# One tile per PSUM bank, and the MLP's side work dealt out over more units, in a two-layer fp32 transformer trunk

## The chip, the cores and the metric

One core of a Trainium2 chip runs the whole program once. The metric is the device time of that execution in microseconds (us), lower is better. TensorE (PE) multiplies, with its weight loads shown apart (PEld); VectorE (DVE), ScalarE (ACT) and GpSimd (POOL) do elementwise work; SyncE (SP) issues every DMA from one queue in the order written.

## The reference, cut to what matters

256 rows of width 2048 pass a forgetting attention (layer A), a squared-ReLU MLP, a shared key/value projection, a chunked attention with a relative bias (layer B) and a second MLP. All arithmetic is float32.

```python
def sq_relu_mlp(h, g, w1, w2):
    a = jax.nn.relu(rms_norm(h, g) @ w1)      # (256, 2048) @ (2048, 8192)
    return (a * a) @ w2                       # (256, 8192) @ (8192, 2048)

h = h + o.reshape(B, S, D) @ a_w_out[l]       # layer A: attention, then
h = h + sq_relu_mlp(h, mlp_norm_g[layer], mlp_w1[layer], mlp_w2[layer])
kv = rms_norm(h, kv_norm_g) @ kv_w            # shared K/V for layer B
q = (rms_norm(h, b_norm_g[l]) @ b_w_q[l])     # layer B: queries, attention, and an MLP as above
```

## The kernel before

**Units and splits.** Every weight is cut into units of 128x1024 floats: two slices of 128 input rows for 512 output columns. A unit is loaded into `raw` (four buffers), and split in `issue` into a rounded part `hi` (ACT, L183) and the rest `lo` (DVE, L184). `three` (L391 to L393) multiplies activations, split likewise, in three products: x.hi with w.hi, x.hi with w.lo, x.lo with w.hi. A unit serves 2 slices x 2 row blocks x 3 products, 12 matmuls. `hi` and `lo` have three buffers each, so when PE starts unit i, the split of unit i+2 may begin, and must be over when unit i+1 ends.

**Pairs and forms.** The MLP takes its weight columns in pairs of 1024 (halves a and b, units a0 to a7 and b0 to b7) and a chunk of 2048 hidden features at a time: chunk 0 to 3, each with two pairs of w1 and two of w2. All pairs but each MLP's first replace units 0 and 1 of both halves by seven combined units, the forms f0 to f6 (a Strassen-like product): the weights 11, T3, T2, T1, 21, T4, 22 in this order, with T1 = 12 - 11, T3 = 22 - 12, T2 = T3 + 11, T4 = 21 - T2. `bring` loads the four raw weights, `make` forms the sums on DVE (L754). A form is 6 matmuls. A pair's forms are dealt among units: f0, the last three units b5 b6 b7 of the pair before, then its own, as in f0 b5 f1 b6 f2 b7 f3 a2 f4 a3 f5 a4 f6 a5 ... b4. The form f1's product is copied to SBUF by ACT as `p` (L789), f0's to another accumulator (L786), and DVE adds `p` back twice (L767 after f2, L775 after a2). Each pair holds four PSUM banks: one pair of banks is always `acc`, the other alternately `acc` and `s`. An `acc` pair is one tile over two banks; `s` tiles have a bank each. The framework keeps order by tile: who writes a tile waits for those who still read it.

**The side work.** `fill` is a list with an entry for each unit to come (forms have none): `run_fill` runs an entry's steps after that unit's matmuls have been issued. Each 512 hidden columns, n = 0 to 3 in a chunk, go this way: after the half's last unit DVE turns the PSUM blocks into `z` (L280), SP writes `z` to DRAM (`rows`, L290) and reads it back in four parts (`columns`, L296), ACT applies ReLU (L700), squares into `hi` (L704), squares again in place (L706), DVE subtracts (L707). For n = 0, `sums` then makes the activation sums that the forms need: four DVE operations (L243 to L248), two rounded parts on ACT (L240) and two remainders on DVE (L241). Entries are counted from the unit after the one that ended the half.

**Order.** `keep_order` fixes each engine's order (DVE, ACT, PE, SP) as the code was written; nothing is reordered to fill a wait. An operation that waits holds up all behind it on its engine.

The same `sums` and `split_turned` (L257, L260, L261) split the normalised rows in `next_x` after the two output projections (stage oa and ob) and before the second layer's projections (stage qb), where `again` makes a second split for K/V.

Of the kernel before, what the change touches and what calls it, by code (L numbers as in the profile page):

```python
# [9 lines left out]
F32 = mybir.dt.float32  # L10
F32R = mybir.dt.float32r
AF = mybir.ActivationFunctionType
ALU = mybir.AluOpType
# [33 lines left out]
def trunk(ctx: ExitStack, tc: tile.TileContext, xT, xr, gs, hg, bf, wgate, w_in, w_oa, w1a, w2a,  # L47
# [159 lines left out]
    def acc_pair(which=None):  # L207
        if which is None:
            which, turns[0] = turns[0], 1 - turns[0]
        if which == 2:  # L210
            return [ps_s.tile([P, 512], F32, name="s") for _ in range(2)]
        t = ps_acc.tile([P, 2 * 512], F32, name="acc", tag=f"acc{which}", bufs=1)
        return [t[:, i * 512 : (i + 1) * 512] for i in range(2)]

    part = [None]

# [13 lines left out]
    def sums(a, fs):  # L230

        w = [wk.tile([P, 512], F32, name="sum", tag="wk") for _ in range(2)]

        def part(i):
            v = w[i // 2][:, i % 2 * 256 : i % 2 * 256 + 256].rearrange("p (g t) -> p g t", g=2)
            return v.rearrange("p g (i c) -> p g i c", i=4) if len(a[0][0].shape) == 4 else v

        def parts(i):
            hi, lo = (fs[k][:, i * 512 : (i + 1) * 512] for k in range(2))
            S.activation(hi, w[i], AF.Copy)  # L240
            V.tensor_tensor(lo, w[i], hi.bitcast(F32), op=ALU.subtract)  # L241

        V.tensor_tensor(part(0), a[1][0], a[1][1], op=ALU.add)  # L243
        V.tensor_tensor(part(1), part(0), a[0][0], op=ALU.subtract)
        parts(0)
        yield
        V.tensor_tensor(part(2), a[0][0], a[1][0], op=ALU.subtract)
        V.tensor_tensor(part(3), a[0][1], part(1), op=ALU.subtract)  # L248
        parts(1)
        yield  # L250

    def split_turned(t, n, which, into, fs=None):
# [51 lines left out]
    def next_x(n, r2, stats, which, into, kept=None, fs=None):  # L304
        add_h = residual(n, r2)
        zt = []
        fs = fs if n == 0 else None

        def use(flipped=False, which=which, into=into):
            t = zt[1].rearrange("p (i k b c) -> p k b i c", i=4, k=GH, b=NB)  # L310
            if flipped:
                t = t[:, :, :, ::-1, ::-1]
            return split_turned(t, n, which, into, fs)

        def turn():
            zt.extend(turned("s" if kept is not None and n >= 2 else "q"))
            for b in range(NB):
                blocks32(h[b][:, n * 512 : (n + 1) * 512], zt[0], b)

        def f(b, ps):  # L320
            add_h(b, ps)
            if b == NB - 1:
                step = steps(use)
                add_fill([[lambda b=b: stats.add(b, n) for b in range(NB)], [turn],
                          [lambda: add_fill(carry(*zt) + [[]] + [[step]] * (2 if fs is None else 4))]])
                if kept is not None:
                    kept.append(use)
        return f
# [101 lines left out]
        for e in evacs[2 if woven else 0 :]:  # L430
            panels(x, [e])

    def head_norm(stats, z, dst, late=0, copied=False):
        rest = []

        def f(b, ps):
            src = ps
            if copied:
                src = wk.tile([P, 512], F32, name="qc", tag="wk")
                V.tensor_copy(src, ps)  # L440
            sq = wk.tile([P, 512], F32, name="sq", tag="wk")
            S.activation(sq, src, AF.Square)
            ss = sm.tile([P, GH], F32, name="ss")
            rn = sm.tile([P, GH], F32, name="rn")

            def total():
                V.tensor_reduce(ss, sq.rearrange("p (a d) -> p a d", a=GH), axis=AX.X, op=ALU.add)

            def norm():
                vv = sm.tile([P, GH], F32, name="vv")  # L450
                V.tensor_scalar(vv, ss, 1.0 / P, stats().e[:, b : b + 1], op0=ALU.mult, op1=ALU.add)  # L451
                G.tensor_tensor(rn, vv, mhalf, op=ALU.pow)  # L452

            def turn():
                qn = wk.tile([P, 512], F32, name="qn", tag="wk")
                V.tensor_tensor(qn.rearrange("p (a d) -> p a d", a=GH), src.rearrange("p (a d) -> p a d", a=GH),
                                rn.unsqueeze(2).to_broadcast([P, GH, P]), op=ALU.mult)
                blocks32(qn, z, b)

            rest.append((total, norm, turn))  # L460
            if b == NB - 1:
                for total, norm, _ in rest:
                    total()
                    if not late:
                        norm()
                add_fill([[]] * (late - 1) + ([[n for _, n, _ in rest]] if late else []) + [[t] for _, _, t in rest] + carry(z, dst))
        return f

    def scale_q(land, layer, g):
# [93 lines left out]
    def add_fill(items):  # L563
        for i, it in enumerate(items):
            if i < len(fill):
                fill[i] = fill[i] + it
            else:
                fill.append(it)
# [126 lines left out]
    def mlp(plan, x, Sx, st, last):  # L695
# [3 lines left out]
        def take(t, c, n):  # L699
            S.activation(t, t, AF.Relu)  # L700
            y = acts.tile([P, 2, GH, T], F32R, name="act")
            hi, lo = (y[:, i].rearrange("p k (b i c) -> p (k b) i c", b=NB, i=4) for i in range(2))
            t3 = t.rearrange("p (i kb c) -> p kb i c", i=4, c=32)
            S.activation(hi, t3, AF.Square)  # L704
            yield
            S.activation(t, t, AF.Square)  # L706
            V.tensor_tensor(lo, t3, hi.bitcast(F32), op=ALU.subtract)  # L707
            hids[c].extend(y[:, :, j, :] for j in range(GH))
            yield
            if n == 0:  # L710
                room = prob.tile([P, 9 * 3 * P], F32R, name="Sh", tag="p", bufs=1)
                Sh[c].extend(room[:, i * GH * T : (i + 1) * GH * T] for i in range(2))
                yield from sums([[t3[:, 2 * j + b :: 4] for j in range(2)] for b in range(NB)], Sh[c])

        def turn_hidden(c, n):
            zt = []

            def f(b, ps):
                if b == 0:
                    zt.extend(turned())  # L720
                blocks32(ps, zt[0], b)
                if b == NB - 1:
                    step = steps(lambda: take(zt[1], c, n))
                    add_fill(carry(*zt)[:3] + [[]] + [[step]] * (4 if n == 0 else 2))
            return f

        pairs = list(dict.fromkeys(p for p, _, _ in plan))
# [1 line left out]
        def open_pair(p):  # L729
            m = pairs.index(p)  # L730
            c, second, r = m // 4, m % 4 >= 2, m % 2
            p.x, p.fs = (hids[c], Sh[c]) if second else (x, Sx)
            p.ps = [acc_pair(0), acc_pair(2 if p.third else 1)]
            if second:
                p.evac = [(last if c == NCH - 1 else residual)(2 * r + q, st.r2) for q in range(2)]
            else:
                p.evac = [turn_hidden(c, 2 * r + q) for q in range(2)]

        def bring(p, name):
            t = qkv.tile([P, UN], F32, name="w" + name, tag="kv"[name[1] == "2"], bufs=2)  # L740
# [12 lines left out]
                        "T2": ("T3", "11", ALU.add), "T4": ("21", "T2", ALU.subtract)}[name]  # L753
            V.tensor_tensor(t[name], t[a], t[b], op=op)  # L754

        ahead = {8: (bring, "12"), 7: (bring, "21"), 6: (bring, "11"), 4: (bring, "22"), 3: (make, "T1"), 2: (make, "T3")}
        starts = [i for i, it in enumerate(plan) if it[1:] == (2, 0)]
        for i, (p, q, u) in enumerate(plan):
            hi, lo = fetch()
# [8 lines left out]
            else:  # L768
# [4 lines left out]
                        p.evac[q](b, p.ps[q][b])  # L773
                if p.fast and (q, u) == (0, 2):
                    V.tensor_tensor(p.ps[1][1], p.ps[1][0], p.t["P7"], op=ALU.add)  # L775
                    make(p, "T4")
                nxt = next((j for j in starts if j > i), None)
                if nxt is not None:
                    d = sum(1 for it in plan[i:nxt] if it[1] < 2)
# [3 lines left out]
            if i and plan[i - 1][1:] in ((2, 0), (2, 1)):  # L783
                f = plan[i - 1][0]
                if plan[i - 1][2] == 0:
                    S.activation(f.ps[0][0], f.ps[1][0], AF.Copy)  # L786
                else:
                    f.t["P7"] = wk.tile([P, 512], F32, name="p7", tag="wk")
                    S.activation(f.t["P7"], f.ps[1][1], AF.Copy)  # L789

    st1, x1, S1 = RowStats("m"), [], []
    stage(o, [next_x(n, None, st1, 1, x1, fs=S1) for n in range(NG)], True)
# [2 lines left out]
    mlp(plan_a, x1, S1, st1, lambda n, r2: next_x(n, r2, st2, 3, xb, kept))  # L795
    xkv = []
    again = [steps(lambda n=n: kept[n](True, 2, xkv)) for n in range(NG)]
    add_fill([[], [], [st2.both], [], [st2.flip]] + [[]] * 13 + [[again[i // 2]] for i in range(2 * NG)])


    qs, evs = [], []
    for g in range(NG):
        box = {}

        def f(b, ps, box=box, g=g):
            if b == 0:
                z, lq = turned("z")
                box["lq"], box["f"] = lq, head_norm(lambda: st2, z, lq, copied=g == 0)
            box["f"](b, ps)
            if b == NB - 1:  # L810
                add_fill([[]] * 7 + [[lambda: qs.append(scale_q(box["lq"], 1, g))]])
        evs.append(f)
    stage(xb, evs, True)
    st2f = st2.flipped
# [90 lines left out]
```

## Time and profile before

| what | us |
|---|---|
| median of 3 runs | 2180.1 (2177.74 to 2183.59) |
| the profiled execution | 2179.85 |
| its span, first to last instruction | 2178.1 |
| PE busy (matmuls) | 2132.4 |
| weight loads busy | 1746.2 |
| DVE busy | 1571.9 |
| ACT busy | 1180.4 |

The profile's page has the busy time of each engine, the chain of waits that ended last, and groups of instructions by line. Its waits name who waited for whom; in the timeline every row has a start, a duration, the engine, the line and in brackets the idle time before it and what ended that. A matmul's row lasts 0.39 us though the next one starts 0.23 us later.

### The profile page before, as it was taken

The numbers are of one execution on the slowest core, as the hardware profiler recorded it, in microseconds if no ns is written. First come the engines' busy times: TensorE is split into PE (matmuls) and PEld (weight loads), VectorE is DVE, ScalarE is ACT, GpSimd is POOL, SyncE is SP. The second block draws the span as 40 slices with busy tenths as digits, with TensorE's granted clock in tenths as the row PEclk, the third lists the DMA queues.
The fourth block names the chain that finished last, engine by engine and source line by source line (L and its number), as shares of the span: only waits on it lengthen the run. The fifth ranks groups of instructions, "written<-read, shape, count | busy, mean of one in ns | idle before, by whom it ended". The sixth has DMA issues, their size and how long they took to land.

```text
span 2178.1 us, 25889 instructions
## 1 busy us (share of the span) xinstructions
PE 2132.4 (98%) x9338; PEld 1746.2 (80%) x9338; DVE 1571.9 (72%) x1795; ACT 1180.4 (54%) x1421; POOL 48.3 (2%) x47
## 2 busy tenths in 40 slices
PE   9999999999999999999999999999999999999999
PEld 7788887878877877878887888878788788778787
DVE  6767766677777777777766677666777777777776
ACT  6544545555465555456656444455655654565554
POOL 1100000000000000000010000000000000000000
PEclk9999999999999999999999999999999999999999
DMA  7777776766665666567668767777665666655664
GB/s 278 240 251 248 226 246 224 251 222 218 228 219 198 211 242 212 191 219 256 204 221 251 239 227 241 235 228 251 224 236 203 206 220 227 219 201 197 226 244 145
DMA packets 183889, 491.62 MB, mean 226 GB/s; under 512 B 36928, under 2 KB 73936, under 8 KB 183760
## 3 DMA queue, kind: packets, MB, share of 16 engines
q1 hardware_dynamic: 183760, 489.96, 66.7%
q8 instruction: 73, 1.20, 0.2%
q14 instruction: 56, 0.46, 0.1%
HBM read 450.01 MB, written 39.87 MB: 225 GB/s over the span
## 4 chain that ended last, share of the span: by engine, by line
PE 82%; DVE 8%; ACT 4%; issue 4%; DMA 2%; SPq 0%; ACTq 0%; DVEq 0%
PE acc L392 22%; PE acc L393 22%; PE acc L391 22%; PE s L392 5%; PE s L393 5%; PE s L391 5%; DVE lo L184 4%; ACT hi L183 2%; DVE z L280 1%; DVE w L754 1%; ACT q L700 1%; PE s L504 1%; PE po L535 1%; DMA z<-turn 1%; ACT p L789 0%
## 5 line engine op out<-in xcount | busy, mean ns | idle before, releaser
L184 DVE TENSOR_TENSOR lo<-raw,hi 128x1024 fp32r<-128x1024 f32 (+1 forms) x650 | 789.2, 1216 | 362.2 <-ACT hi L183 352.3
L183 ACT ACTIVATE hi<-raw 128x1024 fp32r<-128x1024 f32 (+1 forms) x650 | 685.6, 1056 | 523.4 <-PE acc L393 422.8
L391 PE MATMUL acc<-hi,act 128*128 128x512 f32 x2356 | 930.5, 395 | 14.1 <-ACT hi L183 14.1
L392 PE MATMUL acc<-lo,act 128*128 128x512 f32 x2356 | 924.5, 392 | 11.8 <-DVE lo L184 11.2
L393 PE MATMUL acc<-hi,act 128*128 128x512 f32 x2356 | 920.6, 391 | 0.0
L392 PEld LDWEIGHTS acc<-lo,act 128*128 128x128 f32 x2356 | 444.4, 189 | 116.5 <-DVE lo L184 26.1
L391 PEld LDWEIGHTS acc<-hi,act 128*128 128x128 f32 x2356 | 444.5, 189 | 110.6 <-ACT hi L183 18.9
L393 PEld LDWEIGHTS acc<-hi,act 128*128 128x128 f32 x2356 | 444.2, 189 | 92.2 <-DVE act L227 0.3
L183 ACT ACTIVATE hi<-w 128x1024 fp32r<-128x1024 f32 x150 | 159.1, 1061 | 223.1 <-DVE w L754 98.9
L184 DVE TENSOR_TENSOR lo<-w,hi 128x1024 fp32r<-128x1024 f32 x150 | 182.9, 1219 | 65.6 <-ACT hi L183 64.6
L392 PE MATMUL s<-lo,act 128*128 128x512 f32 x416 | 163.8, 394 | 4.3 <-DVE lo L184 4.3
L391 PE MATMUL s<-hi,act 128*128 128x512 f32 x416 | 163.3, 393 | 0.9 <-ACT hi L183 0.9
L393 PE MATMUL s<-hi,act 128*128 128x512 f32 x416 | 163.3, 392 | 0.0
L184 DVE TENSOR_TENSOR lo<-wT,hi 128x1024 fp32r<-128x1024 f32 x60 | 73.4, 1224 | 82.9 <-ACT hi L183 82.9
L183 ACT ACTIVATE hi<-wT 128x1024 fp32r<-128x1024 f32 x60 | 63.5, 1058 | 76.1 <-PE s L393 38.2
L392 PEld LDWEIGHTS s<-lo,act 128*128 128x128 f32 x416 | 79.0, 190 | 21.6 <-DVE lo L184 5.2
L391 PEld LDWEIGHTS s<-hi,act 128*128 128x128 f32 x416 | 78.8, 189 | 18.2 <-ACT hi L183 1.7
L393 PEld LDWEIGHTS s<-hi,act 128*128 128x128 f32 x416 | 79.1, 190 | 16.4
L754 DVE TENSOR_TENSOR wT<-w,w 128x1024 f32<-128x1024 f32 x60 | 73.1, 1218 | 0.0
L452 POOL TENSOR_TENSOR rn<-vv,mhalf 128x4 f32<-128x4 f32 x32 | 42.8, 1352 | 393.7 <-DVE vv L451 393.7
L538 ACT ACTIVATE act<-po 128x256 fp32r<-128x256 f32 x32 | 12.3, 385 | 67.0 <-PE po L536 67.0
L707 DVE TENSOR_TENSOR act<-q,act 128x1024 fp32r<-128x1024 f32 x32 | 39.0, 1220 | 0.5 <-ACT q L706 0.5
(161 smaller groups left out, 1337.0 us busy)
## 6 DMA issues: line engine op xcount, KB each, us to landing
raw<-in_w1a SPq DMA_DIRECT2D x100, 512.0 KB, 4.4
raw<-in_w1b SPq DMA_DIRECT2D x100, 512.0 KB, 4.2
raw<-in_w2a SPq DMA_DIRECT2D x96, 512.0 KB, 4.2
raw<-in_w2b SPq DMA_DIRECT2D x96, 512.0 KB, 4.1
raw<-in_w_in SPq DMA_DIRECT2D x94, 512.0 KB, 4.5
raw<-in_w_kv SPq DMA_DIRECT2D x64, 512.0 KB, 4.2
turn<-z SPq DMA_DIRECT2D x60, 512.0 KB, 4.2
q<-turn SPq DMA_DIRECT2D x168, 128.0 KB, 4.2
```

The costliest lines, as they stand in the source:

```text
L183: S.activation(hi[:, c], raw[:, c], AF.Copy)
L184: V.tensor_tensor(lo[:, c], raw[:, c], hi[:, c].bitcast(F32), op=ALU.subtract)
L280: V.transpose(z.rearrange("p (j n b c) -> p b n j c", j=4, n=n, b=nb)[:, b], src.rearrange("p (n j c) -> p n j c", n=n, j=4))
L391: TE.matmul(ps, xh, wh, start=first, stop=False, **kw)
L392: TE.matmul(ps, xh, wl, start=False, stop=False, **kw)
L393: TE.matmul(ps, xl, wh, start=False, stop=last, **kw)
L452: G.tensor_tensor(rn, vv, mhalf, op=ALU.pow)
L504: TE.matmul(s[:, P : 3 * P], q[:, a, P:T], k[:, a], start=True, stop=True)
L535: TE.matmul(po[:, :T], v[:, 0, a * P : (a + 1) * P], pT[:, :2], start=True, stop=False)
L700: S.activation(t, t, AF.Relu)
L707: V.tensor_tensor(lo, t3, hi.bitcast(F32), op=ALU.subtract)
L754: V.tensor_tensor(t[name], t[a], t[b], op=op)
```

## The change

The instructions are the same, and so are their numbers; only tiles, places in the fill list and the order on DVE, ACT and SP differ.

- `acc_pair` hands out two tiles of one bank where it gave one tile of two.
- `sums` issues its four additions and both ACT roundings in one step and both DVE remainders in the next.
- `take` has four steps (ReLU; square into `hi`; square in place; subtraction) where it had two; `turn_hidden` puts them at entries 3, 4, 6, 7 (n = 0, and its sums at 8, 9), 3 to 6 (n = 1), 3, 4, 6, 7 (n = 2), and 3, 4, 5, 5 (n = 3); before they stood at 4 and 5 (sums at 6, 7). `columns` follows `rows` by one entry, not two.
- `bring` and `make` come earlier, by the number of units before the next pair's f0: 12, 11, 22, 21 at 9 to 6 (were 12, 21, 11, 22 at 8, 7, 6, 4), T1 at 5 (was 3). T4 is made right after the copy of f1's product; it was made after a2 and the second addition of `p`.
- `next_x` moves the sums two entries back and n = 1's split two entries on; K/V's second splits take entries 6 to 22 in place of 18 to 25; the second layer's query group 1 turns two entries later.

```diff
-        t = ps_acc.tile([P, 2 * 512], F32, name="acc", tag=f"acc{which}", bufs=1)
-        return [t[:, i * 512 : (i + 1) * 512] for i in range(2)]
+        return [ps_acc.tile([P, 512], F32, name="acc", tag=f"acc{which}{b}", bufs=1) for b in range(NB)]
...
-        def parts(i):
-            hi, lo = (fs[k][:, i * 512 : (i + 1) * 512] for k in range(2))
-            S.activation(hi, w[i], AF.Copy)
-            V.tensor_tensor(lo, w[i], hi.bitcast(F32), op=ALU.subtract)
-
         V.tensor_tensor(part(0), a[1][0], a[1][1], op=ALU.add)
         V.tensor_tensor(part(1), part(0), a[0][0], op=ALU.subtract)
-        parts(0)
-        yield
         V.tensor_tensor(part(2), a[0][0], a[1][0], op=ALU.subtract)
         V.tensor_tensor(part(3), a[0][1], part(1), op=ALU.subtract)
-        parts(1)
+        hi, lo = ([fs[k][:, i * 512 : (i + 1) * 512] for i in range(2)] for k in range(2))
+        for i in range(2):
+            S.activation(hi[i], w[i], AF.Copy)
+        yield
+        for i in range(2):
+            V.tensor_tensor(lo[i], w[i], hi[i].bitcast(F32), op=ALU.subtract)
         yield
...
-                          [lambda: add_fill(carry(*zt) + [[]] + [[step]] * (2 if fs is None else 4))]])
+                          [lambda: add_fill(carry(*zt) + [[]] * (3 if n == 1 else 1) + [[step]] * 2 + ([] if fs is None else [[], [], [step], [step]]))]])
...
+            yield
             S.activation(hi, t3, AF.Square)
             yield
             S.activation(t, t, AF.Square)
+            yield
             V.tensor_tensor(lo, t3, hi.bitcast(F32), op=ALU.subtract)
...
-                    add_fill(carry(*zt)[:3] + [[]] + [[step]] * (4 if n == 0 else 2))
+                    uses = (4, 5, 6, 6 if late else 7) if n % 2 else (4, 5, 7, 8, 9, 10)[: 6 if n == 0 else 4]
+                    add_fill(carry(*zt, 0)[:2] + [[step] * uses.count(i) for i in range(3, uses[-1] + 1)])
...
-        ahead = {8: (bring, "12"), 7: (bring, "21"), 6: (bring, "11"), 4: (bring, "22"), 3: (make, "T1"), 2: (make, "T3")}
+        ahead = {9: (bring, "12"), 8: (bring, "11"), 7: (bring, "22"), 6: (bring, "21"), 5: (make, "T1"), 2: (make, "T3")}
...
                 if p.fast and (q, u) == (0, 2):
                     V.tensor_tensor(p.ps[1][1], p.ps[1][0], p.t["P7"], op=ALU.add)
-                    make(p, "T4")
...
                     S.activation(f.t["P7"], f.ps[1][1], AF.Copy)
+                    make(f, "T4")
...
-    add_fill([[], [], [st2.both], [], [st2.flip]] + [[]] * 13 + [[again[i // 2]] for i in range(2 * NG)])
+    add_fill([[], [], [st2.both], [], [st2.flip]])
+    slots = {6: 0, 7: 0, 8: 1, 9: 1, 13: 2, 14: 2, 21: 3, 22: 3}
+    add_fill([[again[slots[i]]] if i in slots else [] for i in range(23)])
```

Three places show what moved. The first is DVE in the second pair of w1, chunk 2 of layer A, from f3's split on (f3 splits `wT`; in the rows of before `w_6194` is weight 21 and `w_6226` becomes T4, `w_6268` is 22; a unit's split reads `raw`). Before:

```order
L184 TENSOR_TENSOR lo<-wT_6290,hi 128x1024
L767 TENSOR_TENSOR acc<-s,p_6396 128x512
L184 TENSOR_TENSOR lo<-raw,hi 128x1024
L707 TENSOR_TENSOR act<-q,act 128x1024
L280 STREAM_TRANSPOSE z<-acc 128x4x4x32 x2
L184 TENSOR_TENSOR lo<-w_6194,hi 128x1024
L184 TENSOR_TENSOR lo<-raw,hi 128x1024
L243 TENSOR_TENSOR sum<-q 128x256
L244 TENSOR_TENSOR sum<-sum,q 128x256
L241 TENSOR_TENSOR Sh<-sum,Sh 128x512
L775 TENSOR_TENSOR s<-s,p_6396 128x512
L754 TENSOR_TENSOR w_6226<-w_6194,w_6164 128x1024
```

And now, where 21 is `w_6258`, T4 `w_6196` and 22 `w_6226`, and lines past L209 stand one to four lower (L706 is the subtraction L707, L277 the turn L280):

```order
L754 TENSOR_TENSOR w_6196<-w_6258,w_6166 128x1024
L184 TENSOR_TENSOR lo<-wT_6278,hi 128x1024
L767 TENSOR_TENSOR acc<-s,p_6427 128x512
L184 TENSOR_TENSOR lo<-raw,hi 128x1024
L277 STREAM_TRANSPOSE z<-acc 128x4x4x32 x2
L184 TENSOR_TENSOR lo<-w_6258,hi 128x1024
L184 TENSOR_TENSOR lo<-raw,hi 128x1024
L775 TENSOR_TENSOR s<-s,p_6427 128x512
L184 TENSOR_TENSOR lo<-w_6196,hi 128x1024
L184 TENSOR_TENSOR lo<-raw,hi 128x1024
L706 TENSOR_TENSOR act<-q,act 128x1024
L184 TENSOR_TENSOR lo<-w_6226,hi 128x1024
```

The subtraction, the sums and T4 no longer stand between f3's split and T4's; T4 is made ahead of f3's split.

The second is ACT in the first pair of w2, chunk 2 of layer A, from f1's split (`wT`) on; f2 splits `w_6504`, and f1's product is copied to `p`. Before:

```order
L183 ACTIVATE hi<-wT_6657 128x1024
L183 ACTIVATE hi<-raw 128x1024
L786 ACTIVATE acc<-acc 128x512
L183 ACTIVATE hi<-w_6504 128x1024
L183 ACTIVATE hi<-raw 128x1024
L700 ACTIVATE q<-q 128x1024
L704 ACTIVATE act<-q 128x1024
L789 ACTIVATE p_6744<-acc 128x512
```

And now (L697 is the ReLU L700, L702 the square L704, L785 and L788 the two copies):

```order
L183 ACTIVATE hi<-wT_6692 128x1024
L183 ACTIVATE hi<-raw 128x1024
L697 ACTIVATE q<-q 128x1024
L785 ACTIVATE acc<-acc 128x512
L183 ACTIVATE hi<-w_6495 128x1024
L183 ACTIVATE hi<-raw 128x1024
L702 ACTIVATE act<-q 128x1024
L788 ACTIVATE p_6777<-acc 128x512
```

The ReLU moved ahead of f2's split, so that one pass, not two, stands ahead of the copy to `p`.

The third is DVE at the end of the second pair of w1 in chunk 0, where the sums of n = 0 have moved to (the split of `w_3897` is f0 of the first w2 pair, `wT_4062` its T3; the `raw` split ahead of the sums is b4, the one behind T3 is b5). Now:

```order
L184 TENSOR_TENSOR lo<-raw,hi 128x1024
L706 TENSOR_TENSOR act<-q,act 128x1024
L277 STREAM_TRANSPOSE z<-acc 128x4x4x32 x2
L184 TENSOR_TENSOR lo<-raw,hi 128x1024
L237 TENSOR_TENSOR sum<-q 128x256
L238 TENSOR_TENSOR sum<-sum,q 128x256
L239 TENSOR_TENSOR sum<-q 128x256
L240 TENSOR_TENSOR sum<-q,sum 128x256
L706 TENSOR_TENSOR act<-q,act 128x1024
L184 TENSOR_TENSOR lo<-w_3897,hi 128x1024
L246 TENSOR_TENSOR Sh<-sum,Sh 128x512 x2
L754 TENSOR_TENSOR wT_4062<-w_3928,w_3861 128x1024
```

Before, the sums stood two to three units earlier and one subtraction, the turn and T1 stood between b3's split and f0's; T3 followed f0's split at once. Both subtractions, the sums and their remainders now stand ahead of b5's split.

More of the change, by code (lines that the diff above doesn't have):

```diff
@@ L431, in stage, with head_norm @@
             panels(x, [e])
-    def head_norm(stats, z, dst, late=0, copied=False):
+    def head_norm(stats, z, dst, late=0, copied=False, gap=0):
         rest = []
@@ L465, in f @@
                         norm()
-                add_fill([[]] * (late - 1) + ([[n for _, n, _ in rest]] if late else []) + [[t] for _, _, t in rest] + carry(z, dst))
+                add_fill([[]] * (late - 1) + ([[n for _, n, _ in rest]] if late else []) + [[]] * gap + [[t] for _, _, t in rest] + carry(z, dst))
         return f
@@ L713, in take, with turn_hidden @@
                 yield from sums([[t3[:, 2 * j + b :: 4] for j in range(2)] for b in range(NB)], Sh[c])
-        def turn_hidden(c, n):
+        def turn_hidden(c, n, late):
             zt = []
@@ L736, in open_pair @@
             else:
-                p.evac = [turn_hidden(c, 2 * r + q) for q in range(2)]
+                p.evac = [turn_hidden(c, 2 * r + q, r == 1) for q in range(2)]
         def bring(p, name):
@@ L807, in f @@
                 z, lq = turned("z")
-                box["lq"], box["f"] = lq, head_norm(lambda: st2, z, lq, copied=g == 0)
+                box["lq"], box["f"] = lq, head_norm(lambda: st2, z, lq, copied=g == 0, gap=2 * (g == 1))
             box["f"](b, ps)
             if b == NB - 1:
-                add_fill([[]] * 7 + [[lambda: qs.append(scale_q(box["lq"], 1, g))]])
+                add_fill([[]] * (7 + 2 * (g == 1)) + [[lambda: qs.append(scale_q(box["lq"], 1, g))]])
         evs.append(f)
```

## The prediction

> **What bounds the kernel now.** First the page: the busy times, and the chain that ended last by engine.
>
> ```profile
> span 2178.1 us, 25889 instructions
> PE 2132.4 (98%) x9338; PEld 1746.2 (80%) x9338; DVE 1571.9 (72%) x1795; ACT 1180.4 (54%) x1421; POOL 48.3 (2%) x47
> PE 82%; DVE 8%; ACT 4%; issue 4%; DMA 2%; SPq 0%; ACTq 0%; DVEq 0%
> ```
>
> PE carries the chain, but 12% of it lies on DVE and ACT: at some places PE waits for a split. How much is there to win? The busy row is a poor guide, since rows overlap; the pace is a better one. In the timeline of PE in an undisturbed stretch these two rows stand nine matmuls apart:
>
> ```profile
> 769.65 0.39 PE L391 MATMUL acc<-hi,act 128*128 128x512 f32 x1
> 771.69 0.39 PE L391 MATMUL acc<-hi,act 128*128 128x512 f32 x1
> ```
>
> 2.04 / 9 = 0.227 us each, so a unit of 12 takes 2.72 and a form of 6 takes 1.36. All 9338 matmuls at that pace would be 2117; that is my estimate of the floor, 61 below the span, and a few us too high where the attention's matmuls are shorter. The Trainium skill, page "Perfetto Trace Analysis", section "Identifying the Most-Contended Engine", says likewise that matmul busy time is no good measure of the distance to roofline because matmuls are pipelined. By the busy row only 2178.1 - 2132.4 = 45.7 could be won, which would stop the gain at 2134; the trace agrees with the page, since rows of 0.39 start 0.227 apart.
>
> Next, PE's waits over the whole span (us in total, times, longest):
>
> ```profile
> PE acc L391 <- ACT hi L183: 14.1, 9, 2.1
> PE acc L392 <- DVE lo L184: 11.2, 18, 1.0
> PE acc L391 <- ACT p L789: 8.1, 8, 1.0
> ```
>
> Few and large: the timeline places nearly all of them at the same units of every chunk. A stall's price below is the distance between two starts less 0.227, which holds the restart too.
>
> **Site A, f2 of the first w2 pair, 8 times.** PE and ACT, chunk 2 of layer A:
>
> ```profile
> 828.83 0.39 PE L393 MATMUL s<-hi,act 128*128 128x512 f32 x1
> 830.23 0.50 PE L391 MATMUL acc<-hi,Sh 128*128 128x512 f32 x1 [1.01 <-ACT p L789]
> ```
> ```profile
> 825.23 1.06 ACT L183 ACTIVATE hi<-w 128x1024 fp32r<-128x1024 f32 x1 [1.17 <-PE s L393]
> ...
> 827.55 1.05 ACT L700 ACTIVATE q<-q 128x1024 f32<-128x1024 f32 x1
> ...
> 829.60 0.58 ACT L789 ACTIVATE p<-acc 128x512 f32<-128x512 f32 x1
> ```
>
> f2 writes one bank of the acc tile; f1's product sits in the other, and its copy stands behind two passes of the fill list. f2's own split (825.23 on ACT, DVE's part right behind) was over more than 2 us before. With a tile per bank f2 waits for that split alone. Its price: 1.40 - 0.227 = 1.17, and 0.1 for the restart (shown at B); the eight waits of the table above confirm the count. **8 x 1.27 = 10.2.** What hides the ReLU, now ahead of that split, is the 1.17 that ACT idles there for PE; without that cover f2's split would be 1.05 later, still ahead of its need. Next late is the first accumulator's copy, on which nothing of the next two forms hangs.
>
> **Site B, f5 of the second w1 pair, chunks 1 to 3 of both layers, 6 times.** PE, then DVE:
>
> ```profile
> 794.90 0.39 PE L393 MATMUL acc<-hi,act 128*128 128x512 f32 x1
> 797.37 0.50 PE L391 MATMUL acc<-hi,act 128*128 128x512 f32 x1 [2.09 <-ACT hi L183]
> 798.63 0.50 PE L392 MATMUL acc<-lo,act 128*128 128x512 f32 x1 [0.76 <-DVE lo L184]
> 798.97 0.40 PE L393 MATMUL acc<-hi,act 128*128 128x512 f32 x1
> ```
> ```profile
> 787.54 1.22 DVE L707 TENSOR_TENSOR act<-q,act 128x1024 fp32r<-128x1024 f32 x1
> ...
> 792.14 0.42 DVE L243 TENSOR_TENSOR sum<-q 128x256 f32<-128x256 f32 x1
> ...
> 793.72 0.69 DVE L241 TENSOR_TENSOR Sh<-sum,Sh 128x512 fp32r<-128x512 f32 x1 [0.70 <-ACT Sh L240]
> ...
> 794.93 1.22 DVE L754 TENSOR_TENSOR w<-w,w 128x1024 f32<-128x1024 f32 x1
> ```
>
> T4 is made last of all, behind the subtraction (1.22), a first addition of the sums and a second (0.42 each), a wait (0.70) and a remainder (0.69). Now T4 stands ahead of f3's split and these items, 3.45 us, come later; the stall is 2.24 + 1.03 + 0.11 = 3.38, and T4's own 1.22 leaves the place too. **6 x 3.38 = 20.3.** What DVE does later than before is late next: it has 28% of the span idle, and the sums stand at entries 8 and 9, where nothing of the same pair follows. T4 needs 21, whose load goes out one unit later (6 ahead of f0, not 7) while T4 comes some three units earlier; six units are 16 us, and the slowest landing quoted under the moved DMAs is 9.8, so I take it as landed. If DVE had no room later, the same 3.45 would stop another unit; that is the first rival.
>
> **The clock.** Behind such a stall PE can run at half pace. At two places of chunk 0 (rows under site C) and four of the six of B, rows are 0.63 long and 0.427 apart. The column behind the five engines is the granted clock:
>
> ```profile
> 462.00:473.00 11.00, 8.42 (x24) 6.12 (x23) 9.00 (x10) 4.33 (x5) 0.00 (x0) 0.69 0.62 207
> 972.00:984.00 12.00, 11.19 (x41) 8.83 (x42) 8.54 (x9) 6.39 (x8) 0.00 (x0) 0.86 0.76 246
> 1543.00:1554.00 11.00, 8.40 (x30) 6.29 (x30) 9.55 (x10) 5.64 (x7) 0.00 (x0) 0.84 0.58 201
> ```
> ```profile
> core 0: 2178.1 us, clock 0.994
> ```
>
> The mean of 0.994 gives 0.006 x 2178.1 = 13.1 us lost in all, to which chunk 0's two windows add 0.31 x 11 + 0.16 x 11 = 5.2. The other **7.9** I put to B and take as won with its stalls. It is the softest term: some of the low clock falls into the idle time itself, so it could be 5.
>
> **Site C, b4 and b5 at the end of chunk 0's second w1 pair, twice.**
>
> ```profile
> 462.61 0.39 PE L393 MATMUL s<-hi,act 128*128 128x512 f32 x1
> 463.43 0.51 PE L391 MATMUL s<-hi,act 128*128 128x512 f32 x1 [0.44 <-ACT hi L183]
> 466.08 0.79 PE L392 MATMUL s<-lo,act 128*128 128x512 f32 x1 [2.14 <-DVE lo L184]
> 466.67 0.63 PE L393 MATMUL s<-hi,act 128*128 128x512 f32 x1
> 467.09 0.63 PE L391 MATMUL s<-hi,act 128*128 128x512 f32 x1
> ```
> ```profile
> 460.06 0.42 DVE L247 TENSOR_TENSOR sum<-q 128x256 f32<-128x256 f32 x1
> ...
> 465.94 1.22 DVE L754 TENSOR_TENSOR wT<-w,w 128x1024 f32<-128x1024 f32 x1
> 467.07 1.22 DVE L184 TENSOR_TENSOR lo<-w,hi 128x1024 fp32r<-128x1024 f32 x1
> ```
>
> Before: 0.82 - 0.227 = 0.6, and 2.65 - 0.227 = 2.4, twice: 6.0, with 5.2 of clock 11.2. Here the change does not clear DVE, it regroups it. In the order now, behind b3's split, stand the subtraction, the turn, b4's split, four additions, the other subtraction, f0's split, two remainders and T3, all ahead of b5's split. Full rows of DVE start 1.13 apart (465.94 to 467.07), so: five of them (both subtractions, b4, f0, T3) 5.65, the turn about 1.2, four additions of 0.42 1.7, two remainders about 1.2, b5's split 1.2: 11.0. b3's split may begin when a7 starts, three units ahead of b4: 462.83 (462.61 + 0.227) - 3 x 2.72 = 454.7; with 1.06 on ACT, 1.23 on DVE and something queued it is over at about 457.4. Adding 11.0 and 0.5 of waiting for ACT gives 468.9; b5's remainder is needed when b4, f0 and one matmul are through: 462.83 + 2.72 + 1.36 + 0.23 = 467.1, so 1.8 late. I take 2.0 with its restart, twice 4.0, and half of the old clock loss, 2.6. Before less after: 11.2 - 6.6 = **4.6**. Both ends: no gain at all (the same backlog with another name, 0) and all of it (11.2). Page "TensorE: Matmul & The Clock Gate" of the Trainium skill, section "HAM oscillation", says that the clock is halved by idle gaps above about 3.4 us. By that rule a stall of 2 costs no clock and the sum would be 2.6 lower, 2129; the rows here show it halved behind gaps of 2.4 and 2.24, neither near 3.4, so I don't build on it.
>
> **Sites E and F, next to the attention.** PE's waits in units 5 and 6 of the last output projection (each layer), then in query group 2 and group 3 of layer B, four windows:
>
> ```profile
> PE acc L392 <- DVE lo L184: 1.5, 2, 0.9
> ```
> ```profile
> PE acc L392 <- DVE lo L184: 1.5, 2, 1.0
> ```
> ```profile
> PE acc L392 <- DVE lo L184: 0.9, 2, 0.8
> ```
> ```profile
> PE acc L392 <- DVE lo L184: 1.3, 2, 1.0
> ```
>
> The sums come two entries earlier and n = 1's split two later, so the first two waits for `lo` go, **3.0**; what those units wait for `hi` stays. The second splits of K/V spread over 16 entries and take the 0.9 and 1.3 with them: **2.2**; a second split's remainder now stands ahead of another unit's there, so it could be nothing.
>
> **Moved DMAs.** SP issues `columns` right behind `rows`, and waits for these to land:
>
> ```profile
> 767.79 0.33 SPq L290 DMA_DIRECT2D turn<-z  x1
> 772.42 1.75 SPq L296 DMA_DIRECT2D q<-turn  x4
> DMA to landing us min/median/max: 1.7/4.1/9.8
> ```
>
> Before, SP waited too: `columns` went out at 772.42, 4.6 behind `rows`. What is queued behind on SP is a weight load; one entry more of blocking is at most 2.72, and `raw` has four buffers, so a load has a unit or more to spare. I cost it at nothing; without that cover each of 32 turns could be 2.72 late, 87 at the worst, the far end of the last rival. The rest (places of 12, 11, 22, T1) moves 1.22 us operations into the idle DVE: nothing, or a microsecond each where it meets a split.
>
> **Sum**, from the profiled execution's 2179.85 (0.25 below the median): 10.2 + 20.3 + 7.9 + 4.6 + 3.0 + 2.2 = 48.2, so 2131.7, **2132**. A measurement of this kernel tells about 0.3%, 6.5 us, from no change. My range for this case alone is 2123 to 2142: downward the 6.6 that C leaves and 2 of what stays at E, upward the soft terms, 2.9 of clock, 4.6 of C and 2.2 of F.
>
> **Rivals.**
> - *The backlog moves.* DVE keeps the same work, and some 14 sites (one in each of two pairs of 7 chunks) end about 1 us late in place of A and B, with 8 us of clock: 2131.7 + 14 + 8 = 2154 (2142 to 2165). For it: C shows how full DVE can be. Against: the work moved away, 3.45 and T4's own 1.22, is more than the stall.
> - *All goes, chunk 0 too.* If b5's split comes 2 us earlier than I reckon (T3 or a subtraction finding an earlier gap), 6.6 more falls away and with the rest of E the time nears the floor: 2117 and 1.75 outside the span, 2119 (2112 to 2123, as the floor is an upper estimate).
> - *It doesn't do what it says.* f2 still waits for the copy through another tie, and the backlog ahead of T4 stops f6 instead of f5: A, B, the clock and C stay, only E and F are won, 2175 to 2180.
> - *Slower: columns land late.* ACT's ReLU waits for the four parts and holds f2's split, queued behind it, at 14 sites. The split has a unit and a form of room, 4.08, and half of the 1.17 that ACT idles ahead of it, so the last part may land up to 4.7 us behind its issue. The median of 4.1 is inside; at 7 it costs 14 x 2.3 = 32, and clock 14 x 1.7 = 24 (0.14 x 12 at each site): 56 against a gain of 48.2, so 2188. It decides from 4.7, with nearly all landings above; 1.7/4.1/9.8 speaks against that.
>
> **How the numbers follow.** Forecast 0.55, backlog 0.20, all goes 0.15, no gain 0.05, slower 0.05. The range takes in the first three but for the backlog's upper part: 2112 to 2158. Faster by over 0.3% hold the first three, 0.90; within it 0.05; slower 0.05.
>
> **What would show it.** A: no PE wait for the copy to `p`. B: f5's first row 0.23 behind its neighbour in six chunks, and T4's row ahead of f3's split. Clock: windows of chunks 1 to 3 at 1.00, the core at about 0.999. C: a wait of some 2 us at b5 near 450 to 465 of the span, and half-pace rows behind one of the two. It would be wrong if PE waited for `hi` at f2, with ACT's ReLU waiting for a DMA ahead of it, or if new waits for `lo` stood at one unit of every chunk.

## The result and the profile after

The changed kernel takes 2125.6 us (median of 4 runs, 2124.61 to 2125.99), a ratio of 0.9749 to the kernel before, 95% interval 0.9732 to 0.9765: 54 us less. The forecast was 2132, range 2112 to 2158. In what follows one execution, of e10, ran in a slower state (2959 us at a granted clock of 0.67) and is left out of its figure.

The page of the changed kernel, busy times and chain:

```profile
span 2124.2 us, 25852 instructions
PE 2109.3 (99%) x9338; PEld 1740.9 (82%) x9338; DVE 1574.4 (74%) x1795; ACT 1185.6 (56%) x1421; POOL 48.2 (2%) x47
PE 93%; DVE 3%; DMA 1%; ACT 1%; issue 1%; SPq 0%; ACTq 0%; DVEq 0%
```

DVE's and ACT's busy times are what they were (1571.9 and 1180.4 before); their share of the chain fell from 12% to 4%. No work was saved, only moved out of PE's way; the 37 instructions fewer in all are semaphore instructions. The clock, and all of PE's waits that are left:

```profile
core 0: 2124.2 us, clock 1.000
```
```profile
PE acc L389 <- DVE lo L184: 4.8, 7, 1.1
PE s L389 <- DVE lo L184: 3.7, 4, 1.8
PE pt L88 <- DVE mhalf L90: 1.2, 1, 1.2
PE acc L390 <- DVE act L226: 0.4, 1, 0.4
PE s L388 <- DVE acc L767: 0.4, 2, 0.2
```

The waits for `hi` (14.1) and for the copy `p` (8.1) are gone, those for `lo` went from 16.7 (11.2, and 5.5 in `s` tiles) to 8.5. Site A, chunk 2 of layer A, PE and then ACT:

```profile
813.84 0.39 PE L390 MATMUL s<-hi,act 128*128 128x512 f32 x1
814.07 0.39 PE L388 MATMUL acc<-hi,Sh 128*128 128x512 f32 x1
```
```profile
809.18 1.06 ACT L697 ACTIVATE q<-q 128x1024 f32<-128x1024 f32 x1 [0.60 <-DMA q<-turn]
810.14 0.58 ACT L785 ACTIVATE acc<-acc 128x512 f32<-128x512 f32 x1
810.66 1.04 ACT L183 ACTIVATE hi<-w 128x1024 fp32r<-128x1024 f32 x1
...
812.56 1.05 ACT L702 ACTIVATE act<-q 128x1024 fp32r<-128x1024 f32 x1
813.51 0.58 ACT L788 ACTIVATE p<-acc 128x512 f32<-128x512 f32 x1
```

f2 starts 0.23 behind its neighbour. The copy to `p` ends at 814.09, only 0.02 after f2's start: with the passes where they are now, the tie would have cost next to nothing at f2. And the ReLU waits for its columns, with f0's copy and f2's split behind it. Both points come back below.

Site B, the same chunk, DVE and then PE at f5's start:

```profile
771.64 1.22 DVE L754 TENSOR_TENSOR w<-w,w 128x1024 f32<-128x1024 f32 x1
...
779.76 0.69 DVE L775 TENSOR_TENSOR s<-s,p 128x512 f32<-128x512 f32 x1
781.33 1.23 DVE L184 TENSOR_TENSOR lo<-w,hi 128x1024 fp32r<-128x1024 f32 x1 [0.88 <-ACT hi L183]
```
```profile
783.89 0.39 PE L390 MATMUL acc<-hi,act 128*128 128x512 f32 x1
784.12 0.39 PE L388 MATMUL acc<-hi,act 128*128 128x512 f32 x1
```

T4 is made at 771.64, its split runs at 781.33, and f5 starts at 784.12 without a wait. Site C, chunk 0 of layer A, PE and DVE:

```profile
468.29 0.39 PE L388 MATMUL s<-hi,act 128*128 128x512 f32 x1
470.03 0.50 PE L389 MATMUL s<-lo,act 128*128 128x512 f32 x1 [1.35 <-DVE lo L184]
```
```profile
463.21 0.42 DVE L240 TENSOR_TENSOR sum<-q,sum 128x256 f32<-128x256 f32 x1
463.55 1.22 DVE L706 TENSOR_TENSOR act<-q,act 128x1024 fp32r<-128x1024 f32 x1
465.27 1.23 DVE L184 TENSOR_TENSOR lo<-w,hi 128x1024 fp32r<-128x1024 f32 x1 [0.51 <-ACT hi L183]
466.42 1.29 DVE L246 TENSOR_TENSOR Sh<-sum,Sh 128x512 fp32r<-128x512 f32 x2
467.62 1.22 DVE L754 TENSOR_TENSOR wT<-w,w 128x1024 f32<-128x1024 f32 x1
468.76 1.22 DVE L184 TENSOR_TENSOR lo<-raw,hi 128x1024 fp32r<-128x1024 f32 x1
```

This stall remains, 1.74 - 0.227 = 1.5 us (2.0 in layer B), at b5 as forecast. Behind it the clock stays up, the window says (the column behind the five engines):

```profile
464.00:475.00 11.00, 9.65 (x43) 7.68 (x42) 9.96 (x10) 7.43 (x9) 0.00 (x0) 1.00 0.50 151
```

**A ledger.** For each trace the distances between the starts of L391 to L393's matmuls (their lines in that kernel), less 0.227, are added up by stage wherever they exceed 0.015 (behind the attention's smaller matmuls, less the usual distance of these). This is what PE lost there, half-pace matmuls included. Times are those of the profiled executions.

| kernel | time | w1 pair 2, chunks 1-3 (B) | the same, chunk 0 (C) | w2 pair 1 (A) | oa3, ob3 (E) | qb (F) | first two attention stages | rest | sum |
|---|---|---|---|---|---|---|---|---|---|
| before | 2179.85 | 30.3 | 11.4 | 13.8 | 5.5 | 4.9 | 3.2 | 10.0 | 79.0 |
| changed | 2125.99 | 0 | 6.2 | 0.2 | 1.4 | 2.0 | 5.6 | 9.9 | 25.2 |
| e1 tiles | 2183.49 | 33.7 | 10.9 | 11.7 | 7.7 | 3.4 | 4.8 | 9.8 | 81.9 |
| e3 T4 | 2156.09 | 10.4 | 12.0 | 10.2 | 5.6 | 2.5 | 3.5 | 10.0 | 54.2 |
| e4 passes | 2149.09 | 3.4 | 6.8 | 11.9 | 7.9 | 2.3 | 6.0 | 10.0 | 48.2 |
| e5 rows | 2176.58 | 33.2 | 9.9 | 13.0 | 0 | 2.0 | 5.7 | 11.6 | 75.4 |
| e10 passes, tiles | 2142.06 | 3.3 | 7.0 | 2.2 | 8.0 | 4.8 | 5.9 | 9.8 | 41.0 |
| e11 T4, tiles | 2149.71 | 10.6 | 11.4 | 2.3 | 5.9 | 3.5 | 4.2 | 10.0 | 48.0 |
| e2 changed, one tile | 2128.17 | 0 | 6.1 | 4.2 | 1.4 | 2.0 | 3.6 | 10.0 | 27.4 |
| e6 changed, T4 back | 2127.71 | 3.3 | 5.1 | 1.6 | 1.4 | 2.0 | 4.3 | 9.8 | 27.5 |
| e9 columns +1 | 2128.48 | 0 | 8.6 | 2.2 | 1.4 | 2.0 | 3.9 | 9.8 | 27.9 |
| e7 columns +2 | 2281.55 | 51.4 | 31.6 | 80.3 | 1.4 | 2.0 | 3.3 | 9.8 | 179.7 |
| e8 sums in three | 2119.34 | 0 | 3.2 | 0 | 1.4 | 2.0 | 2.5 | 9.8 | 18.9 |
| e12 the same again | 2123.2 | 0 | 3.2 | 0 | 1.4 | 2.0 | 6.4 | 9.8 | 22.9 |

79.0 - 25.2 = 53.8, and the times differ by 53.86: the ledger holds the whole difference. The first two attention stages vary by 4 us between two executions of one kernel (2.5 and 6.4 in the last two rows), so differences of that size there belong to no edit. Each row is one execution, and half-pace rows differ between executions of one kernel too: the granted clock of the kernel before is 0.991 to 0.996 over its executions.

### The profile page after: what moved, and what is told of

Read it like the earlier page. It is cut to its first block, busy times and chain, and to the rows that moved or that the text cites. A ratio compares the mean times of both kernels' runs of the same rounds, so it can differ in the third digit from the quotient of the medians.

```text
span 2124.2 us, 25852 instructions
## 1 busy us (share of the span) xinstructions
PE 2109.3 (99%) x9338; PEld 1740.9 (82%) x9338; DVE 1574.4 (74%) x1795; ACT 1185.6 (56%) x1421; POOL 48.2 (2%) x47
## 4 chain that ended last, share of the span: by engine, by line
PE 93%; DVE 3%; DMA 1%; ACT 1%; issue 1%; SPq 0%; ACTq 0%; DVEq 0%
PE acc L390 25%; PE acc L389 25%; PE acc L388 25%; PE s L389 6%; PE s L390 6%; PE s L388 6%; DVE lo L184 1%; DMA raw<-in_w_in 1%; ACT hi L183 1%; PE po L532 1%; PE s L501 1%; PE po L533 0%; PE s L500 0%; DVE wT L754 0%; DVE z L277 0%
## 5 line engine op out<-in xcount | busy, mean ns | idle before, releaser
L389 PEld LDWEIGHTS acc<-lo,act 128*128 128x128 f32 x2356 | 442.4, 188 | 102.1 <-DVE lo L184 10.9
L536 DVE TENSOR_TENSOR act<-po,act 128x256 fp32r<-128x256 f32 x32 | 13.6, 424 | 34.4 <-ACT act L535 34.4
```

The lines of the kernel that those rows point to most:

```text
L389: TE.matmul(ps, xh, wl, start=False, stop=False, **kw)
L536: V.tensor_tensor(o[i][:, 1], po[:, :T], o[i][:, 0].bitcast(F32), op=ALU.subtract)
```

## The experiments

### Each part alone

**e1, two tiles only** (a `-` line is the kernel before):

```diff
-        t = ps_acc.tile([P, 2 * 512], F32, name="acc", tag=f"acc{which}", bufs=1)
-        return [t[:, i * 512 : (i + 1) * 512] for i in range(2)]
+        return [ps_acc.tile([P, 512], F32, name="acc", tag=f"acc{which}{b}", bufs=1) for b in range(NB)]
```

> The kernel before with one edit: acc_pair hands out two tiles of one bank. Theory: the wait at f2 of the first w2 pair (site A) was a tie through the two-bank tile alone, so its eight waits for the copy to p vanish with nothing else moved: w2p0 lost 13.6 us in the profile of before over its eight chunks, all stalls counted, so 2166 to 2170; sites B and C stay as they are. Rival: the ReLU and the square ahead of the copy hold f2 in another way too (its own split, or the addition of p), then 2178 or more.

Measured 2181.63 us, ratio 0.9999 (0.9990 to 1.0009): no gain at all. The wait at f2 did go, as the theory had it, but three forms later stands a new one. PE and DVE of e1:

```profile
833.85 0.39 PE L392 MATMUL s<-hi,act 128*128 128x512 f32 x1
834.08 0.39 PE L390 MATMUL acc<-hi,Sh 128*128 128x512 f32 x1
...
846.71 0.50 PE L390 MATMUL acc<-hi,act 128*128 128x512 f32 x1
847.97 0.50 PE L391 MATMUL acc<-lo,act 128*128 128x512 f32 x1 [0.76 <-DVE lo L184]
```
```profile
843.65 0.70 DVE L774 TENSOR_TENSOR acc<-acc,p 128x512 f32<-128x512 f32 x1
844.25 1.22 DVE L753 TENSOR_TENSOR w<-w,w 128x1024 f32<-128x1024 f32 x1
846.69 1.23 DVE L184 TENSOR_TENSOR lo<-w,hi 128x1024 fp32r<-128x1024 f32 x1 [1.21 <-ACT hi L183]
```

f2 no longer waits 1.17, and f5 waits 1.26 - 0.227 = 1.03 for T4's split. The stall at f2 had given DVE and ACT time to catch up; without it T4, made last, is late. The ledger's A column falls only from 13.8 to 11.7. B and E stand 3.4 and 2.2 higher in this trace, in half-pace rows and longer waits; whether the edit did that is open.

**e3, T4 and the loads and T1 ahead of it only** (these were not tried apart here; e6 moves T4 alone):

```diff
-        ahead = {8: (bring, "12"), 7: (bring, "21"), 6: (bring, "11"), 4: (bring, "22"), 3: (make, "T1"), 2: (make, "T3")}
+        ahead = {9: (bring, "12"), 8: (bring, "11"), 7: (bring, "22"), 6: (bring, "21"), 5: (make, "T1"), 2: (make, "T3")}
...
                 if p.fast and (q, u) == (0, 2):
                     V.tensor_tensor(p.ps[1][1], p.ps[1][0], p.t["P7"], op=ALU.add)
-                    make(p, "T4")
...
                     S.activation(f.t["P7"], f.ps[1][1], AF.Copy)
+                    make(f, "T4")
```

> The kernel before with T4 and the loads and T1 of the next pair moved (the table ahead and make T4 behind the copy), nothing else. Theory: T4's own place wins the wait for hi at f5 (2.24 us) but the subtraction, the sums and the addition still stand ahead of f5's split on DVE, so PE waits there for lo, 0.9 to 2.1 us at six sites: 10 to 20 us gained of the 28 that B and its clock cost, 2160 to 2170. Rival 1: T4 alone is enough, all 28 gained, 2150 to 2153. Rival 2: the passes are what matters and T4's place nothing: 2178 to 2182.

2156.06 us, ratio 0.9885 (0.9870 to 0.9899), a little better than the theory's range. B falls from 30.3 to 10.4. What stays at each of the six sites is a wait for `lo` at f5, 0.83, just under the 0.9 to 2.1 expected, and smaller stalls at f6 (0.43) and f4 (0.07), with their restarts.

**e4, passes and sums only** (the hunks of `sums`, `take` and `turn_hidden`):

```diff
-                    add_fill(carry(*zt)[:3] + [[]] + [[step]] * (4 if n == 0 else 2))
+                    uses = (4, 5, 6, 6 if late else 7) if n % 2 else (4, 5, 7, 8, 9, 10)[: 6 if n == 0 else 4]
+                    add_fill(carry(*zt, 0)[:2] + [[step] * uses.count(i) for i in range(3, uses[-1] + 1)])
```

> The kernel before with the passes and sums moved (take, turn_hidden, sums), but the two-bank tile, T4, the table ahead and the row splits as before. Theory: these clear DVE ahead of f5, so T4 at its old place (behind the second addition, which ends at 780.45 in the changed kernel's trace, f5 due at 784.12) is in time: B and its clock (28 us), nearly all of A (11) and 5 of C are won, 2134 to 2140. Rival: T4's place is needed as well, B keeps a stall of 1 to 2 us at six sites with some half-pace clock: 2148 to 2160.

2148.6 us, ratio 0.9848 (0.9832 to 0.9865). The theory missed by 9 us, and the rival's figure is met for another reason: B is nearly gone (3.4 of 30.3), T4's place is not needed for it. The loss is at f1 of the first w2 pair, in PE's waits of e4:

```profile
PE acc L389 <- ACT acc L787: 8.1, 6, 2.6
```

f1 writes one bank of the acc tile, and the copy of f0's product reads the other. That copy now stands behind a ReLU that waits for its columns: the tie through the two-bank tile, moved from f2 to f1.

**e5, the splits of the normalised rows only** (the hunks of `next_x`, `again`, and the query group's `gap`):

```diff
+    slots = {6: 0, 7: 0, 8: 1, 9: 1, 13: 2, 14: 2, 21: 3, 22: 3}
+    add_fill([[again[slots[i]]] if i in slots else [] for i in range(23)])
```

> The kernel before with the edits of next_x, the second K/V splits and the turn of query group 1 alone. Theory: sites E and F only: output projections lost 5.5 us and query groups 4.9 in the profile of before, 1.4 and 2.0 in that of the changed kernel, so 7 us: 2171 to 2175. Rival: E needs the regrouped sums too (not in this kernel), so only 3 to 4: 2175 to 2178.

2175.14 us, ratio 0.9974 (0.9963 to 0.9985), on the edge of the theory. E is gone (5.5 to 0), F 4.9 to 2.0; 1.6 of new loss stands in the stage behind E (0.8 at the first unit of each MLP), so some 4 of E's 5.5 are won.

### Parts together

**e10, passes and two tiles** (the diffs of e1 and e4).

> The kernel before with the moved passes and sums and the two tiles of one bank, T4 and the rest as before. With the passes alone (2148.6) PE waits at f1 of the first w2 pair, 8.1 us in six waits, for the copy of f0's product, which stands behind a ReLU that waits for its columns; f1 writes the other bank of the same tile. Theory: that tie is the tile's, so with two tiles the six waits and their restarts and clock (10.5 us of loss in w2p0, against 0.2 in the changed kernel) go: 2137 to 2141. Rival: f1's own split stands behind the same ReLU and is just as late: 2145 to 2149.

2139.59 us, ratio 0.9807 (0.9789 to 0.9826), as the theory had it: A falls from 11.9 to 2.2, and no wait for the copy is left.

**e11, T4 and two tiles** (the diffs of e1 and e3).

> The kernel before with the early T4 (and the table ahead) and the two tiles, passes as before. Two tiles alone gained nothing (2181.6): the wait at f2 went, but as much came back at f5 of the same pair, which waits for T4's split. Theory: with T4 made early f5 is not late, and the two tiles now win what f2 loses, 8 x 1.28 us of the 2156.1 that T4 alone gives: 2144 to 2148. Rival: the backlog on ACT and DVE only moves on to f3 to f6: 2153 to 2157.

2150.14 us, ratio 0.9852 (0.9834 to 0.9871). A falls from 10.2 to 2.3; the time falls by 6 against 10 expected, since in this trace the query groups lose 1.0 more, the first attention stages 0.7 (within what they vary by), and each chunk still loses 0.3 in A. The rival's figure is not met. So the same edit, worth nothing alone, is worth some 6 to 9 us beside an early T4 or beside the moved passes.

### One part taken back

**e2, the changed kernel with the tile of two banks** (e1's diff reversed).

> The changed kernel with the two-bank tile of before. Theory: with the ReLU moved ahead of f2's split the copy to p ends at 814.09 in the changed kernel's trace, 0.02 us after f2's start, so the tie costs only 0.1 to 0.4 us at each of eight sites: 2127 to 2129; the tile and the moved pass each do for the same stall. Rival: the tile is what wins A, and without it its 10 to 13.6 us come back: 2136 to 2139.

2129.66 us, ratio 0.9763 (0.9748 to 0.9777), near the theory and far from the rival. The tile's own share at the end is 2 to 4 us, but not at f2 as the theory had it: A stands 4.0 higher, mainly in waits of 0.2 to 0.7 at f1 in four of the chunks, for f0's copy. In e4, with the same passes and the same tile, f1 waited 8.1 us in all, here 1.4. Between the two kernels lie T4, the loads and T1 ahead of it, and the row splits; e6, which has the loads early and T4 late, loses only 1.6 in A. This points to the places of the loads, but e6 has the two tiles, and no run moves the loads alone, so it is not shown.

**e6, the changed kernel with T4 at its old place** (the last two hunks of e3 reversed).

> The changed kernel with T4 made at its old place, behind a2 and the second addition of p. Theory: with the passes moved DVE reaches T4 at about 780.4 of the changed kernel's trace and f5 is due at 784.12, so nothing is lost: 2125 to 2127. Rival: T4's place is a part of B's gain, and 6 sites lose 1 to 3.4 us each: 2132 to 2150.

2127.06 us, ratio 0.9752 (0.9738 to 0.9767): the theory. What e3 gained by 26 us, e6 loses by 1.5 (0.7 by the ratios), within the intervals; passes and T4 clear the same place. Its trace does show a small price that the theory put at nothing: 0.55 at a6, two units after f6, in each of the six pairs, 3.3 in all.

### How near the slower rival is

**e7, columns two entries later** and **e9, one entry later** (as in the kernel before); e9 has `carry(*zt, 1)` and `i < 4`:

```diff
-                    add_fill(carry(*zt, 0)[:2] + [[step] * uses.count(i) for i in range(3, uses[-1] + 1)])
+                    move = carry(*zt, 2)
+                    add_fill([(move[i - 1] if i < 5 else []) + [step] * uses.count(i) for i in range(1, uses[-1] + 1)])
```

> The changed kernel with the four column reads issued two entries later (two weight loads then stand between them and the row write on SP), ReLU where it was. This puts a price on the slower rival of the prediction. In the changed kernel's trace the ReLU starts 0.02 to 0.1 us behind the last landing at many turns of n = 0 and n = 2, so a later landing holds ACT at once. Theory of the prediction's rival: 1 to 2.2 us later, against a room of 4.7 counted from the issue with a landing of 4.1: 14 sites lose about 1.4 each and 24 us of clock, 2160 to 2175. Other theory: the split behind the ReLU has 1.3 to 2.4 us of room of its own (f2's split ends at 812.96, f2 reads it at 814.3), so little is lost: 2126 to 2132.

> The changed kernel with the column reads one entry later, as far behind the row write as in the kernel before. Theory, from the run with two entries: a weight load that stands between rows and columns on SP waits until a raw buffer is free, and holds the columns; with one load between it waits at most about a unit (2.7 us) longer than the rows take to land, and ACT's ReLU, which starts 0.02 to 0.1 us behind the last landing at most turns of n = 0 and n = 2 already, is held by 1 to 2.7 us at 16 turns. The split behind it has about 2 us of room, so 2126 to 2135. Rival: there is no room, and 32 turns lose 2 to 3 us each with clock: 2190 and more. Second rival: SP waits for the rows in both cases, nothing changes: 2124 to 2127.

e9 takes 2128.04 us, ratio 0.9752 (0.9737 to 0.9767): within its theory, not distinct from the changed kernel by the times, though the ledger's A and C are 4.4 higher together and the ReLU's waits for columns rise from 1.7 us to

```profile
ACT q L697 <- DMA q<-turn: 21.5, 19, 3.2
```

e7 takes 2281.31 us, ratio 1.0454 (1.0437 to 1.0472). Both of its theories were far too mild. SP, ACT and PE of e7, in order:

```profile
820.61 0.33 SPq L287 DMA_DIRECT2D turn<-z  x1
...
830.55 4.67 SPq L171 DMA_DIRECT2D raw<-in_w1a  x2
835.27 1.85 SPq L293 DMA_DIRECT2D q<-turn  x4
```
```profile
841.18 1.06 ACT L697 ACTIVATE q<-q 128x1024 f32<-128x1024 f32 x1 [6.63 <-DMA q<-turn]
842.14 1.04 ACT L183 ACTIVATE hi<-raw 128x1024 fp32r<-128x1024 f32 x1
```
```profile
843.24 0.50 PE L388 MATMUL s<-hi,act 128*128 128x512 f32 x1 [2.79 <-ACT hi L183]
```
```profile
ACT q L697 <- DMA q<-turn: 197.7, 32, 10.0
```

Here the columns go out 14.7 us behind the rows. Between them on SP stand seven loads, not two; four go into `raw`, and each of these goes out when a split on DVE has freed its buffer (the last at 834.89). At 14 of the 32 turns, those of n = 1 and 3 in all but the first pair, it is so, with 13.0 to 14.7 us; in e9 four loads and 6.3 to 6.9 us stand there, in the changed kernel two loads and 4.0 to 5.0. At n = 0 and 2 of the later chunks e7 has two loads and 6.4 to 7.7 us. The splits behind the ReLU on ACT wait with it, and PE waits for them. That the late splits then hold the next loads in turn (the `raw` load behind these columns goes out at 844.47, after the split that stood behind the ReLU) is likely to add to it; how much is not shown, for the splits that freed the buffers ahead of these columns all ran before that ReLU. One entry costs little, the second 153 us more.

### What is left of site C

**e8 and e12, sums in three steps,** the roundings and remainders an entry later in chunk 0:

```diff
         hi, lo = ([fs[k][:, i * 512 : (i + 1) * 512] for i in range(2)] for k in range(2))
+        yield
         for i in range(2):
...
-                    uses = (4, 5, 6, 6 if late else 7) if n % 2 else (4, 5, 7, 8, 9, 10)[: 6 if n == 0 else 4]
+                    uses = (4, 5, 6, 6 if late else 7) if n % 2 else (4, 5, 7, 8, 9, 9 + (c == 0), 10 + (c == 0))[: 7 if n == 0 else 4]
```

(In `next_x` two of the steps share an entry, so that nothing moves there.)

> The changed kernel with sums in three steps (additions; roundings; remainders), the roundings and remainders one entry later in chunk 0 only; elsewhere the three fall on the same entries as now. It aims at what is left of site C: b5 waits 1.5 and 2.0 us for its remainder. ACT's rounding for f0's split then no longer waits behind the sums' roundings (462.99 to 464.30 in the changed kernel's trace, the split's at 464.20), and the two remainders (1.2 us) come behind b5's split. Theory: both stalls go, 3.5 us: 2121 to 2123. Rival: the backlog only moves on to f1 or f2, with 1 to 3 us of stall there: 2124 to 2128.

> The kernel with sums in three steps once more, in five rounds, to say whether it is below the changed kernel (2125.6; ratio 0.9749). Theory: the two stalls at b5 are gone in its trace, 3.5 us, and the ratio to before is 0.972 to 0.974, 2120 to 2123. Rival: the first figure of 2120.9 was chance, and it comes out at 0.9745 to 0.976.

2120.94 and 2122.9 us, ratios 0.9726 (0.9712 to 0.9741) and 0.9727 (0.9712 to 0.9742). Both traces have no wait at b5; DVE of e8 shows why:

```profile
461.20 1.23 DVE L184 TENSOR_TENSOR lo<-w,hi 128x1024 fp32r<-128x1024 f32 x1
462.34 1.23 DVE L755 TENSOR_TENSOR wT<-w,w 128x1024 f32<-128x1024 f32 x1
463.47 1.23 DVE L184 TENSOR_TENSOR lo<-raw,hi 128x1024 fp32r<-128x1024 f32 x1
464.61 1.29 DVE L247 TENSOR_TENSOR Sh<-sum,Sh 128x512 fp32r<-128x512 f32 x2
```

f0's split no longer waits for ACT, and the remainders stand behind b5's split, not ahead. C falls from 6.2 to 3.2: the 3.7 of b5 (with its restarts) is gone, and 0.35 comes back at b6 in each layer, far from the rival's 1 to 3. The interval overlaps that of the changed kernel, so by the times alone it is about 0.2% ahead, with the trace as the firmer evidence.

## Why the prediction came out right, by its own steps

- **Size.** 48.2 was forecast, 54 measured. By the ledger: B with its clock 28.2 forecast, 30.3 found; A 10.2 against 13.6; C 4.6 against 5.2; E 3.0 against 4.1; F 2.2 against 2.9; the first attention stages took back 2.4. A was mis-sized: of its 13.8 before, 0.8 were half-pace rows behind C, and each chunk lost 1.62 in that pair, where only f2's 1.27 was counted; the other 0.34 stood at f5. In E the waits for `hi` were said to stay, and they went.
- **A's step was wrong in its cause.** It read "with a tile per bank f2 waits for that split alone" and gave the 10.2 to the tile. e1 shows that this edit alone gains nothing, e4 that the moved passes alone leave 11.9 of the 13.8, e10 and e11 that the tile wins it beside the passes or beside an early T4, and e2 that the rest of the change wins 9.6 of the 13.6 without the tile. The 10 us are real in the whole change, and that the term came out near its size although its cause was wrong is luck: the change holds several edits that do for the same stall. Also, "next late" was named wrongly: not f0's copy, "on which nothing of the next two forms hangs", but T4's split (e1); and f0's copy did hold f1 where the passes had moved and the tile still had two banks (e4, e2).
- **B** was right in mechanism: items ahead of T4 on DVE. Passes and T4 were summed as one; e3 and e4 show that either wins most (20 and 27 of 30.3), so they overlap.
- **C** was forecast at b5, 1.8 us late; measured 1.5 and 2.0. Half of the clock loss was kept, and none came; a new stall at f3 of the same pair took back 0.4 in each layer. The 0.8 at f2, the same in both kernels, was not in the prediction's sum.
- **The backlog rival** fell for the whole change, but it is just what e1 shows, and in part e3.
- **The slower rival** has the right chain (columns, ReLU, the split behind it) and a wrong price: its 4.7 us of room was counted for a late landing, while e7's columns were held on SP behind loads. One late landing is on record: in e6, chunk 1 of layer B (n = 2), the last part lands 7.0 us behind the first issue, the ReLU waits 2.97 for it, and f2 then waits for its split; that pair loses 1.6 with no half-pace row, where the rival put 2.3 and 1.7 of clock. In the changed kernel's chunk 2 the split ends at 812.96 and f2 reads it at 814.29, 1.3 us to spare. What kept the change clear of the rival is that columns follow rows with no load between at these turns, and with two in place of three at n = 1 and 3. SP then waits longer for the rows, which cost nothing: of the changed kernel's waits on SP,

```profile
SPq L293 <- DMA turn<-z: 105.1, 51, 5.2
```

against 48.1 in 28 waits before.

The four parts alone gain 0, 26, 33 and 6 us, 65 in all; together 54. A sum of parts is no proof of any one of them.

## What to carry to other kernels

When a stall goes, follow the engines that had been catching up in it: ask what they are late for next, and take the stall's price as won only if that has room. Where two edits clear the same backlog, price them together and test them apart. And on a queue that issues in order, put between two transfers of one chain as few transfers as possible that themselves wait for a buffer.

## What the runs showed of the hardware that had not been expected

Half pace can follow waits that stand close together, none of them long. Over the MLP and projection stages of all these traces, stalls (the distance between two starts less 0.227) above 0.4 us whose rows start less than 2.5 us apart were added up, and it was counted how often at least four matmuls some 0.43 apart came behind: sums of 1.0 to 1.9 us, 0 of 65; 1.9 to 2.5, 14 of 29; 2.5 to 3.3, 18 of 22; above 3.3, 19 of 20. (The bound is 0.4 because the first slow row behind a restart is itself some 0.36 late.) In e10's query group 3 stalls of 0.62 and 1.31 did it. The same stall went both ways (2.42 at b4: half pace at one of e5's two sites, not at the other). The Trainium skill, page "TensorE: Matmul & The Clock Gate", section "HAM oscillation", warns of idle gaps above about 3.4 us; here sums of 1.9 to 3.3, which hold no gap of that length, did it in 32 of 51 cases. Between 1.0 and 1.9 us no sum did.
